# A two-block transformer kernel: modulation in column quarters, attention heads scored in pairs, weights divided ahead of plain transposes

## The chip, the cores and the metric

The kernel runs on one NeuronCore of a Trainium2 chip, as one launch. The metric is the device time of that launch in microseconds. The core has a matrix engine (TensorE, in the profile PE for products and PEld for loading their stationary operand), three engines for elementwise work (VectorE or DVE, ScalarE or ACT, GpSimd or POOL), a queue engine (SyncE or SP) that issues most transfers, and 16 DMA engines. All engines run at the same time and meet at semaphores. Operands lie in SBUF (128 partitions), products land in PSUM: eight banks of 512 fp32 columns for each partition.

## The reference, cut to what matters

Two transformer blocks follow one another, each on 256 tokens of an image (`x`) and 256 of a context (`ctx`) of width 1024. All data is fp32.

```
mod = silu(c) @ w_ada + b_ada                       # (1024) @ (1024 x 9*1024): shift, scale, gate, three times; twice 6*1024 in the second model
h   = rmsnorm(x, g) * (1 + scale) + shift
x   = x + 0.5 * gate * rmsnorm(swiglu(h), g)        # FFN 1, for x and for ctx

# mixer of the first block: window attention (8 heads, 2 key heads, 256 own + 256 context keys) and a gated scan in both directions
s = q @ k.T * 64**-0.5                              # windows of 128 masked
p = softmax(concat(s_band, s_ctx, sink))            # the sink has no value row
o = p @ v
y = (sigmoid(ga) * (o @ w_o_attn) + sigmoid(gh) * (readout(scan) @ w_o_hgrn)) @ w_out

# second model, layer 0: RWKV-7 scans and latent attention (8 heads of 96) on context, then on x; MoE of 16 experts
# second model, layer 1: grouped-query attention (16 heads of 64, 4 key heads) of 256 queries on 512 keys; MoE
p = softmax(q @ k.T * scale);  o = p @ v;  x = x + gate * (o @ w_out)
```

## The kernel before, in words

Weights are read from HBM once, in pieces of 512 KB (`w_raw`, 128 partitions x 1024 fp32 columns, four buffers in most phases). Most products are made with more than one fast product: an operand is split into a rounded part and a remainder (`split`: ScalarE writes `w_hi`, VectorE or POOL writes `w_lo`), and three products of the fast type fp32r are summed in PSUM (`mm3`, L226 to L230). Products that are written with plain fp32 operands (`mm`, L214) are issued as two instructions each.

The phases in order of time are: `p1` with `ab1` inside it (FFN 1 of the first model for context and x, all its modulation, and beside it the RWKV and latent attention of the context in the second model), `p2` (the first mixer: projections, HGRN and window attention as four streams), `p3` (FFN 2), `ab0` (RWKV and latent attention of x, and the modulation of the last layer beside them), a first MoE, `gq` (grouped-query attention), a second MoE.

Streams are Python generators. In `p1`/`ab1`, `p2` and `ab0` they are advanced one step at a time in an order written out by hand as a string (`ORDERS`, where `T` is a step of the filling work, FFN and modulation). Inside that order a planner of the framework places the instructions on the engines by a simulated timeline. On the chip, TensorE and SyncE's queue run theirs in order.

**Modulation** (`ada`, L380 to L413): the vector silu(c) is put into `aT`, 128 x 8 x 32 with two columns in use (x and context). A group of 2048 columns is computed into one PSUM bank: four chunks of 512 columns go to the four strips of 32 partitions (`ps[32 * c:32 * c + 32]`). For each of eight blocks of 128 rows of the weights, two tiles of 1024 columns are loaded, and each tile feeds two chunks. After the eighth block the group is handed over: VectorE adds the bias (`ada_m`), four DMAs write rows to HBM, TensorE transposes four blocks, VectorE copies them (`mt_...`), and bias rows for the next group are loaded into the one buffer `biasr`. The stream has one PSUM buffer (`sm=1`) in `p1`, two in `ab0`. The matrix of 9216 columns makes five groups, the last half full, and each of 6144 makes three: 11.

**Attention** (`attend`, L635 to L687) serves three callers: window attention (`window` in `mixer1`, 8 heads, 512 keys), latent attention (`mla`, 8 heads, once with 256 keys and once with 512), grouped-query attention (`gqa`, 16 heads, 512 keys). For each head and each of two query tiles, `weights` makes scores `at_s` in PSUM by three fp32r products, the maximum `at_mx` (VectorE), the exponential `at_p` with its sum (ScalarE), the reciprocal `at_rd` (VectorE) and a diagonal matrix of it (`diag`, VectorE). `turned` makes, one step later, `at_p` transposed and divided in one go: a product of each 128x128 block with the diagonal (`at_pp`), copied by ScalarE to `at_pt`. After the second tile of an odd head, the values of two heads are summed in `po`, and split into `o_t`.

In window and grouped-query attention a key head holds 64 of the 128 partitions, so its scores are products of 64 rows, in the upper or lower half of the array.

`gq` has four PSUM buffers of one bank each for `acc` and four for `sm`.

Of the kernel before, what the change touches and what calls it, by code (L numbers as in the profile page):

```python
# [132 lines left out]
class _Net:  # L133
    def __init__(self, tc, io, dbg=None):
        self.tc, self.nc, self.io, self.dbg = tc, tc.nc, io, dbg or {}
        self.slots = None
        self.fill = self.wx = None
        self.wn = {"raw": 0, "hi": 0}
# [228 lines left out]
    @contextlib.contextmanager  # L367
    def modulating(self):

        with self.pool("adp", side="right") as self.adp:  # L370
            self.biasr = self.adp.tile([128, 512], F32, name="biasr")
            self.nc.gpsimd.memset(self.biasr, 0.0)
            self.aT = [self.adp.tile([128, 8, 32], F32, name=f"aT{i}") for i in range(2)]
            for i, a in enumerate(self.aT):
                self.nc.vector.memset(a, 0.0)
                self.cp(a[:, :, 0:2], self.vT[:, i * 16:i * 16 + 16].rearrange("p (v k) -> p k v", v=2))
            yield


    def ada(self, pool, which, w, bias, boff, ncols, tag, groups):  # L380


        rows = self.dram([2, ncols], F32, f"ada_{tag}")
        for g in range((ncols + 2047) // 2048):
            c0 = g * 2048
            nch = min(4, (ncols - c0) // 512)
            ps = self.sm()
            for k in range(8):
                raws = []
                for c2 in range(nch // 2):  # L390
                    raw = self.w_raw(2, 512)
                    self.dma(raw.rearrange("p a b -> p (a b)"), w[k * 128:(k + 1) * 128, c0 + c2 * 1024:c0 + (c2 + 1) * 1024])
                    raws.append(raw)
                for c in range(nch):
                    self.mm(ps[32 * c:32 * c + 32, :], self.aT[which][:, k, :], raws[c // 2][:, c % 2, :], k == 0, k == 7)
                if k < 7:
                    yield
            for c in range(nch):
                self.dma(self.biasr[32 * c:32 * c + 2, :], _rep(bias, 2, boff + c0 + c * 512, 512))
            m = self.adp.tile([128, 512], F32, name="ada_m", bufs=1)  # L400
            n = nch * 32
            self.tt(m[:n], ps[:n], self.biasr[:n], OP.add)
            if n < 128:
                self.nc.vector.memset(m[n:], 0.0)
            for c in range(nch):
                self.dma(rows[:, c0 + c * 512:c0 + (c + 1) * 512], m[32 * c:32 * c + 2, :])
            t = pool.tile([128, 4, 4, 2], F32, name=f"mt_{tag}{g}")
            pt = self.sm()
            for blk in range(4):
                self.tr(pt[:, blk * 128:(blk + 1) * 128], m[:, blk * 128:(blk + 1) * 128])  # L410
            self.cp(t, pt.rearrange("p (b c r) -> p b c r", b=4, c=4)[:, :, :, 0:2])
            groups.append((rows, t))
            yield  # L413
# [10 lines left out]
    def pre(self, groups, jshift, jscale, v, gcol):  # L424
        def mod_T(j):
            g, s = divmod(2 * j, 4)
            return groups[g][1][:, :, s:s + 2, v].rearrange("p b c -> p c b")
        gs, sh = self.t(8, name="pre_gs"), self.t(8, name="pre_sh")
        self.cp(sh.rearrange("p (c b) -> p c b", c=2), mod_T(jshift))
        self.stt(gs.rearrange("p (c b) -> p c b", c=2), mod_T(jscale), 1.0,  # L430
                 self.vT[:, gcol:gcol + 8].rearrange("p (c b) -> p c b", c=2), OP.add, OP.mult)
        return gs, sh

    def gate(self, groups, j, v, post=None, scale=1.0, out=None):

        if out is None:
            out = self.t(1024, name="gate")
        rows = groups[0][0]
# [196 lines left out]
    def attend(self, npair, q_of, k_of, v_of, nk, scale, o_t, ok, sink=None, mask=None):  # L635
        nkt = nk // 128

        def weights(h, qt):

            s = self.acc("at_s")  # L640
            self.mm3(s[:, :nk], q_of(h, qt), k_of(h), True, True)
            if mask is not None:
                c0, m = mask(qt)
                self.tt(s[:, c0:c0 + 128], s[:, c0:c0 + 128], m, OP.add)
            mx = self.t(4, name="at_mx")
            self.red(mx[:, 0:1], s[:, :nk], OP.max)
            if sink is not None:
                self.ts(mx[:, 0:1], mx[:, 0:1], scale, sink[:, h:h + 1], OP.mult, OP.max)
                self.ts(mx[:, 1:2], mx[:, 0:1], -1.0, None, OP.mult)
            else:  # L650
                self.ts(mx[:, 1:2], mx[:, 0:1], -scale, None, OP.mult)
            p = self.t(512, name="at_p")
            self.act(p[:, :nk], s[:, :nk], AF.Exp, scale=scale, bias=mx[:, 1:2], accum_out=mx[:, 2:3])
            if sink is not None:
                self.act(mx[:, 3:4], sink[:, h:h + 1], AF.Exp, bias=mx[:, 1:2])
                self.tt(mx[:, 2:3], mx[:, 2:3], mx[:, 3:4], OP.add)
            rd = self.t(1, name="at_rd")
            self.nc.vector.reciprocal(out=rd, in_=mx[:, 2:3])
            return p, self.diag(rd)
        pts = {}  # L660

        def turned(h, qt, p, dg):

            pr, par = divmod(h, 2)
# [6 lines left out]
            if (par, qt) != (1, 1):  # L671
                return
            po = self.sm("po")
            for kt in range(nkt):
                for par in range(2):
                    self.mm(po[64 * par:64 * par + 64, :256], v_of(2 * pr + par, kt), pts[2 * pr + par][:, kt, :], kt == 0, kt == nkt - 1)
            self.split(o_t.pair(ok + pr, 0, 256), po[:, :256])

        was = None
        for h in range(2 * npair):  # L680
            for qt in range(2):
                now = h, qt, *weights(h, qt)
                if was:
                    turned(*was)
                was = now
                yield
        turned(*was)  # L687
# [50 lines left out]
    def mixer1(self, hx, hc, end):  # L738
# [175 lines left out]
        def window():  # L914
# [17 lines left out]
            akT = [self.t(512, dt=F32R, name="akT") for _ in range(2)]  # L932
            self.split(akT, ps)
# [12 lines left out]
            def mask(qt):  # L946
                return (128, self.k["win0"]) if qt == 0 else (0, self.k["win1"])
            yield from self.attend(4, lambda h, qt: [z[64 * (h // 4):64 * (h // 4) + 64, h % 4, qt * 128:(qt + 1) * 128] for z in aqT],
                                   lambda h: [z[64 * (h // 4):64 * (h // 4) + 64, :] for z in akT],
# [462 lines left out]
    def mla(self, ht, keep, is_x, outs):  # L1412
# [126 lines left out]
        yield from self.attend(4, q_of, k_of,  # L1539
# [3 lines left out]
    def gqa(self, ht, hc, x, G):  # L1543
# [79 lines left out]
        for _ in self.attend(8, lambda h, qt: [t[rows(h), h % 4, qt * 128:(qt + 1) * 128] for t in qT[h // 8]],  # L1623
                    lambda h: [t[rows(h), :] for t in kT[h // 8]], lambda h, kt: v[kt][:, h // 4, :], 512, 0.125, o_t, 0):
            pass
        self.proj(o_t, (0, 128), io["gqa_w_out_2"][0], D, [[(0, 512), (512, 512)]], self.gated_to(x, G))
# [278 lines left out]
    def run(self, out):  # L1905
        nc, io = self.nc, self.io
        with contextlib.ExitStack() as es:
# [26 lines left out]
            with self.pool("mods1", side="right") as mods1:  # L1934
# [24 lines left out]
                with self.modulating(), self.pool("zp") as self.zp, self.phase("p1", s=8, h=2, q=2, f=4, b=6, acc=2) as p1:  # L1959
                    ada1 = self.within(self.stream("ada", sm=1), ada1)  # L1960
                    while not m1:
                        next(ada1)
# [14 lines left out]
                    while not m2[0]:  # L1977
                        self.tick()
# [82 lines left out]
    def rest(self, pre2, gate2, x, xc, out, caps, full=None):  # L2061
# [17 lines left out]
        with self.phase("gq" + u, f=17, b=14, q=16):  # L2079

            with self.tc.high_priority(offset=100):
                ht = self.norm_T([(x, lambda: pre2(1, 0, 0))])
            self.gqa(ht, self.norm_T([(xc, lambda: pre2(1, 0, 1))]), x, gate2(1, 0, 0))
            for i in range(2):
                self.dump(f"l1{i}", x[i])
# [33 lines left out]
```

## Time and profile before

| what | value |
|---|---|
| median of three runs | 2508.39 us (2505.49 to 2510.97) |
| profiled execution | 2502.3 us, span 2500.4 us |
| mean granted clock of TensorE | 0.958 of full |
| busy in the span | PE 2287.3, PEld 1795.0, DVE 1448.8, ACT 1151.7, POOL 476.5 us |
| read from HBM | 415.99 MB |

Busy time counts an instruction from its start to its end; products are pipelined, so the starts of two lie closer than one lasts. A line number is that of the listing above, and one that belongs to a helper (L214 for every plain product, L236 for every ScalarE operation) is told apart by the tiles: `out<-in`. "Idle before" is the time in which an engine had nothing to run ahead of these instructions, and what ended it stands behind the arrow.

### The profile page before, as it was taken

To read this page: it belongs to the slowest core of one execution; us is meant where nothing else is said; L and a number is where in the kernel's file an instruction comes from. 1 tells how busy PE (TensorE), PEld (TensorE's weight loads), DVE (VectorE), ACT (ScalarE), POOL (GpSimd) and SP (SyncE) were. 2 spreads that over 40 slices of the span, in tenths; PEclk is the share of its full clock that TensorE was granted. 3 is DMA by queue.
4 is the path that set the end of the run, shared out by engine and by line. 5 is a ranking of instruction groups with operands and counts; after the bars stand their busy time and mean duration, and the time that the engine had idled before them with its cause. 6 is when DMAs were issued, how large, how long until landed. Compare 5 with 4: busy or idle time off the path is not lost. (4 is left out here: it accounts for less than half of the span.)

```text
span 2500.4 us, 42084 instructions
## 1 busy us (share of the span) xinstructions
PE 2287.3 (91%) x16807; PEld 1795.0 (72%) x16807; DVE 1448.8 (58%) x2433; ACT 1151.7 (46%) x1784; POOL 476.5 (19%) x398
## 2 busy tenths in 40 slices
PE   5899999989999989999899899989888978897996
PEld 1686666778888778877799777577676656676774
DVE  1344333466555755786655544554766777547776
ACT  1344223365355434564544453344346754445664
POOL 1132000042000310000100232142225433001342
PEclk9999999999999989999999999989899998898998
DMA  8777776653434433431766556720349983114897
GB/s 275 217 201 235 238 233 226 195 171 119 136 119 135 149 123 101 131 101 45 236 188 185 155 164 197 250 66 18 128 148 340 380 301 105 37 46 152 300 327 245
DMA packets 371414, 445.02 MB, mean 178 GB/s; under 512 B 20928, under 2 KB 273632, under 8 KB 371208
## 3 DMA queue, kind: packets, MB, share of 16 engines
q1 hardware_dynamic: 362280, 409.98, 51.2%
q0 software_dynamic: 4320, 15.47, 1.9%
q10 hardware_dynamic: 4608, 16.78, 1.7%
q8 instruction: 134, 2.20, 0.4%
q14 instruction: 72, 0.59, 0.1%
HBM read 415.99 MB, written 26.96 MB: 177 GB/s over the span
## 5 line engine op out<-in xcount | busy, mean ns | idle before, releaser
L236 ACT ACTIVATE w_hi<-w_raw 128x1024 fp32r<-128x1024 f32 (+2 forms) x550 | 574.8, 1050 | 786.9 <-PE acc L230 313.2
L242 DVE TENSOR_TENSOR w_lo<-w_raw,w_hi 128x1024 fp32r<-128x1024 f32 (+1 forms) x466 | 584.8, 1261 | 457.6 <-ACT w_hi L236 436.1
L228 PE MATMUL acc<-h_h,w_hi 128*128 128x256 f32 (+1 forms) x1392 | 398.0, 286 | 8.0 <-ACT w_hi L236 6.2
L230 PE MATMUL acc<-h_h,w_lo 128*128 128x256 f32 (+1 forms) x1392 | 398.8, 287 | 1.5 <-DVE w_lo L242 0.9
L229 PE MATMUL acc<-h_l,w_hi 128*128 128x256 f32 (+1 forms) x1392 | 390.9, 281 | 0.6 <-POOL h_l L242 0.4
L228 PEld LDWEIGHTS acc<-h_h,w_hi 128*128 128x128 f32 (+1 forms) x1392 | 262.0, 188 | 26.1 <-ACT w_hi L236 10.2
L230 PEld LDWEIGHTS acc<-h_h,w_lo 128*128 128x128 f32 (+1 forms) x1392 | 261.6, 188 | 19.8 <-issue 10.9
L242 POOL TENSOR_TENSOR w_lo<-w_raw,w_hi 128x1024 fp32r<-128x1024 f32 (+1 forms) x84 | 201.9, 2417 | 345.1 <-ACT w_hi L236 331.6
L229 PEld LDWEIGHTS acc<-h_l,w_hi 128*128 128x128 f32 (+1 forms) x1392 | 262.0, 188 | 2.9 <-POOL h_l L242 1.5
L214 PE MATMUL sm<-w_raw,aT 128*32 128x512 f32 x672 | 161.8, 635 | 19.3 <-DMA w_raw<-in_ada_w 8.2
L229 PE MATMUL acc<-w_lo,h_h 128*128 128x512 f32 (+1 forms) x304 | 119.7, 394 | 0.0
L230 PE MATMUL acc<-w_hi,h_l 128*128 128x512 f32 (+1 forms) x304 | 117.1, 390 | 0.0
L229 PE MATMUL acc<-w_lo,mo_e_h 128*128 128x512 f32 x256 | 105.6, 413 | 11.9 <-DVE w_lo L242 11.1
L228 PE MATMUL acc<-w_hi,h_h 128*128 128x512 f32 (+1 forms) x304 | 111.4, 397 | 3.0 <-ACT h_h L236 3.0
L242 POOL TENSOR_TENSOR rs_r<-rs_t,mhalf 128x1 f32<-128x1 f32 (+2 forms) x37 | 38.5, 1041 | 390.8 <-DVE rs_t L246 388.1
L228 PE MATMUL acc<-w_hi,mo_e_h 128*128 128x512 f32 x256 | 104.6, 409 | 3.1 <-ACT w_hi L236 2.5
L229 PE MATMUL acc<-w_lo,f_a_h 128*128 128x512 f32 x264 | 104.8, 403 | 0.0
L228 PE MATMUL acc<-w_hi,f_a_h 128*128 128x512 f32 x264 | 102.9, 412 | 1.7 <-ACT f_a_h L236 1.6
L230 PE MATMUL acc<-w_hi,mo_e_l 128*128 128x512 f32 x256 | 102.2, 399 | 0.0
L230 PE MATMUL acc<-w_hi,f_a_l 128*128 128x512 f32 x264 | 101.3, 397 | 0.0
L214 PEld LDWEIGHTS acc<-ab_Gt,ab_T 64*64 64x64 f32 x1536 | 77.9, 135 | 31.3 <-issue 26.2
L214 PE MATMUL acc<-ab_Gt,ab_T 64*64 64x64 f32 x1536 | 97.7, 224 | 0.0
(542 smaller groups left out, 4471.6 us busy)
## 6 DMA issues: line engine op xcount, KB each, us to landing
w_raw<-in_ffn_w_in SPq DMA_DIRECT2D x132, 512.0 KB
w_raw<-in_ada_w SPq DMA_DIRECT2D x96, 512.0 KB
w_raw<-in_w_ada SPq DMA_DIRECT2D x72, 512.0 KB
w_raw<-in_ffn_w_out SPq DMA_DIRECT2D x66, 512.0 KB
w_raw<-in_moe_w_gate SPq DMA_DIRECT2D x128, 256.0 KB
w_raw<-in_moe_w_up SPq DMA_DIRECT2D x128, 256.0 KB
w_raw<-in_moe_w_down SPq DMA_DIRECT2D x64, 512.0 KB
w_raw<-in_mix_w_in SPq DMA_DIRECT2D x42, 512.0 KB
```

What stands on the lines that cost most here:

```text
L214: self.nc.tensor.matmul(out, lhsT=lhsT, rhs=rhs, start=start, stop=stop, **kw)
L228: mm(out, lhsT=l[0], rhs=r[0], start=start, stop=False)
L229: mm(out, lhsT=l[0], rhs=r[1], start=False, stop=False)
L230: mm(out, lhsT=l[1], rhs=r[0], start=False, stop=stop)
L236: self.nc.scalar.activation(out, in_, f, **kw)
L242: (e or self.nc.vector).tensor_tensor(out=out, in0=a, in1=b, op=op)
```

## The change

Three things are done together. The modulation is computed in groups of 1024 columns, and each weight tile of 1024 columns is cut into four quarters of 256, one for each strip. The buffers and the readers (`pre`, `gate`) follow: group `j` is now the vector `j`, and the places that waited for the first group wait for two. Attention divides the weights by their sum where they lie (`ts` on `at_p`) and turns them with plain transposes in place of products with a diagonal. And `attend` takes a list of pairs of heads and scores them, in grouped-query attention, `together`: both heads of a pair have keys in different halves of the partitions, the scores go to a PSUM tile of two banks (`acc2`), and maximum, scaling and reciprocal are one instruction for two heads. For that the phase `gq` takes two double banks for four single ones, which the projections draw by halves, the pairs of heads are (0,4), (1,5) and so on, and the rows of `w_out` are loaded to match. In window attention each key head gets a tile of its own with the other 64 partitions set to zero, so that its scores are products of 128 rows.

The title of the change also speaks of grouped scan products; no line of the scans (`hgrn`, `rwkv`, `mms`) is in the diff.

```diff
     def acc(self, name="acc"):
+        if self.halves is not None:
+            if not self.halves:
+                t = self.acc2(name)
+                self.halves += [t[:, 1], t[:, 0]]
+            return self.halves.pop()
...
+    def acc2(self, name):
+        p, bufs, tag = self.slots["acc"]
+        return p.tile([128, 2, 512], F32, name=name, tag=tag, bufs=bufs)
...
-        for g in range((ncols + 2047) // 2048):
-            c0 = g * 2048
-            nch = min(4, (ncols - c0) // 512)
+        for g in range(ncols // D):
+            c0 = g * D
             ps = self.sm()
-            for k in range(8):
-                raws = []
-                for c2 in range(nch // 2):
-                    raw = self.w_raw(2, 512)
-                    self.dma(raw.rearrange("p a b -> p (a b)"), w[k * 128:(k + 1) * 128, c0 + c2 * 1024:c0 + (c2 + 1) * 1024])
-                    raws.append(raw)
-                for c in range(nch):
-                    self.mm(ps[32 * c:32 * c + 32, :], self.aT[which][:, k, :], raws[c // 2][:, c % 2, :], k == 0, k == 7)
-                if k < 7:
+            for k in range(0, 8, 2):
+                for kk in range(k, k + 2):
+                    raw = self.w_raw(4, 256)
+                    self.dma(raw.rearrange("p a b -> p (a b)"), w[kk * 128:(kk + 1) * 128, c0:c0 + D])
+                    for c in range(4):
+                        self.mm(ps[32 * c:32 * c + 32, :256], self.aT[which][:, kk, :], raw[:, c, :], kk == 0, kk == 7)
+                if k < 6:
                     yield
...
-            m = self.adp.tile([128, 512], F32, name="ada_m", bufs=1)
+            m = self.adp.tile([128, 256], F32, name="ada_m", bufs=2)
...
-    def attend(self, npair, q_of, k_of, v_of, nk, scale, o_t, ok, sink=None, mask=None):
+    def attend(self, pairs, q_of, k_of, v_of, nk, scale, o_t, ok, sink=None, mask=None, together=False):
...
-            s = self.acc("at_s")
-            self.mm3(s[:, :nk], q_of(h, qt), k_of(h), True, True)
+        def scores(hs, qt):
+            s = self.acc2("at_s") if together else self.acc("at_s")[:, None, :]
+            ops = [(q_of(h, qt), k_of(h)) for h in hs]
+            for n, (a, b) in enumerate(((0, 0), (0, 1), (1, 0))):
+                for z, (l, r) in enumerate(ops):
+                    self.mm(s[:, z, :nk], l[a], r[b], n == 0, n == 2)
...
-            return p, self.diag(rd)
+            for z, p in enumerate(ps):
+                self.ts(p[:, :nk], p[:, :nk], rd[:, z:z + 1], None, OP.mult)
+            return ps
...
-                self.mm(pp[:, kt * 128:(kt + 1) * 128], p[:, kt * 128:(kt + 1) * 128], dg)
+                self.tr(pp[:, kt * 128:(kt + 1) * 128], p[:, kt * 128:(kt + 1) * 128])
...
-            akT = [self.t(512, dt=F32R, name="akT") for _ in range(2)]
-            self.split(akT, ps)
+            akT = [[self.t(512, dt=F32R, name="akT") for _ in range(2)] for _ in range(2)]
+            for z in range(2):
+                r, other = [slice(64 * y, 64 * y + 64) for y in (z, 1 - z)]
+                for k in akT[z]:
+                    nc.gpsimd.memset(k.bitcast(F32)[other], 0.0)
+                self.split([k[r] for k in akT[z]], ps[r])
...
+        pairs = [(8 * z + a, 8 * z + a + 4) for z in range(2) for a in range(4)]
...
-        with self.phase("gq" + u, f=17, b=14, q=16):
+        with self.phase("gq" + u, f=17, b=14, q=16, acc=2):
+            self.halves = []
```

## Rows read from the trace of the kernel before

**Rows 1.** The page's table: busy us (share of the span) x instructions.

```profile
PE 2287.3 (91%) x16807; PEld 1795.0 (72%) x16807; DVE 1448.8 (58%) x2433; ACT 1151.7 (46%) x1784; POOL 476.5 (19%) x398
```

**Rows 2.** Stretches of time: length, busy time by engine, granted clock, DMA share, GB/s.

```profile
0.00:62.00 62.00, 35.03 (x148) 9.96 (x150) 11.56 (x46) 11.32 (x20) 7.67 (x18) 0.92 0.80 275
...
187.00:437.00 250.00, 247.03 (x2098) 165.58 (x2097) 99.92 (x134) 73.52 (x103) 17.12 (x18) 0.99 0.70 233
...
1036.00:1160.00 124.00, 119.25 (x698) 96.90 (x697) 104.64 (x221) 68.41 (x109) 0.53 (x1) 0.96 0.26 83
...
1900.00:2000.00 100.00, 93.44 (x444) 69.10 (x445) 68.85 (x83) 74.67 (x100) 54.16 (x26) 1.00 1.05 380
```

**Rows 3.** Stretches again, TensorE's modulation products alone: busy, clock, DMA, GB/s.

```profile
62.00:500.00 438.00, 94.98 (x384) 0.98 0.70 221
1450.00:1630.00 180.00, 38.37 (x184) 0.98 0.66 210
```

**Rows 4.** Timeline of TensorE: start us, duration us, modulation products and what follows.

```profile
283.89 1.05 PE L214 MATMUL sm<-w_raw,aT 128*32 128x512 f32 x4
284.87 0.27 PE L214 MATMUL sm<-ab_T,ab_Gt 64*64 64x64 f32 x1
...
294.12 1.06 PE L214 MATMUL sm<-w_raw,aT 128*32 128x512 f32 x8
```

**Rows 5.** Waits of SyncE's queue, 187 to 437 us: total, times, longest.

```profile
SPq L211 <- PE sm L214: 105.2, 47, 6.4
```

**Rows 6.** A hand-over on the timeline, and what TensorE waited for before its transposes.

```profile
45.03 0.69 DVE L242 TENSOR_TENSOR ada_m<-sm,biasr 128x512 f32<-128x512 f32 x1 [12.51 <-PE sm L214]
...
46.72 0.64 PE L214 MATMUL sm<-w_raw,aT 128*32 128x512 f32 x4 [0.28 <-DVE mt_a L239]
...
  DVE ada_m L242: 2.7, 2
```

**Rows 7.** Timeline of TensorE in grouped-query attention.

```profile
2161.32 1.94 PE L214 MATMUL po<-at_pt,gq_v 128*64 128x256 f32 x14
...
2163.19 1.16 PE L214 MATMUL at_pp<-diag,at_p 128*128 128x128 f32 x8
2164.28 0.49 PE L228 MATMUL at_s<-gq_kT,gq_qT 64*128 64x512 f32 x1
...
2165.17 1.16 PE L214 MATMUL at_pp<-diag,at_p 128*128 128x128 f32 x8
```

**Rows 8.** Timeline of TensorE: four plain transposes and what follows.

```profile
516.92 0.60 PE L233 MATMUL sm<-tri,mla_q 128*96 128x128 f32 x4
517.45 0.33 PE L214 MATMUL sm<-ab_UV,ab_SC 128*64 128x64 f32 x2
```

**Rows 9.** Timeline of TensorE around one window step (three at_s left out).

```profile
1062.65 0.39 PE L230 MATMUL acc<-w_hi,h_l 128*128 128x512 f32 x1
1062.88 0.40 PE L228 MATMUL acc<-w_hi,h_h 128*128 128x512 f32 x1
...
1064.43 0.39 PE L230 MATMUL acc<-w_hi,h_l 128*128 128x512 f32 x1
```

**Rows 10.** Groups of instructions by form: busy us, mean ns of one | idle before.

```profile
L214 PE MATMUL acc<-ab_lw,ab_lo 64*128 64x512 f32 x16 | 6.9, 861 | 5.0 <-DMA ab_lw<-in_rw_w 4.3 <-DVE ab_sg L242 0.7
```

**Rows 11.** Stretches at the grouped-query stage, columns as in rows 2.

```profile
2134.00:2151.00 17.00, 11.15 (x32) 7.87 (x33) 12.25 (x29) 5.55 (x10) 2.90 (x1) 0.51 0.15 50
2151.00:2232.00 81.00, 81.00 (x472) 56.61 (x471) 35.80 (x131) 43.76 (x102) 0.00 (x0) 1.00 0.01 1
```

**Rows 12.** Stretch by tile (at_pp, then at_s); then min/median/max ns of two scalings.

```profile
2136.00:2232.00 96.00, 37.03 (x256) 31.70 (x256) 18.90 (x32) 0.92 0.02 6
...
2136.00:2232.00 96.00, 32.81 (x96) 17.62 (x96) 21.52 (x32) 24.78 (x64) 0.92 0.02 6
...
L246 DVE TENSOR_SCALAR diag<-tri,at_rd x80: 267/280/830, 552.4 to 2223.0; 128x128 f32<-128x128 f32 x80
...
L246 DVE TENSOR_SCALAR fz<-fz x4: 693/694/695, 956.4 to 959.3; 128x1024 f32<-128x1024 f32 x4
```

More of the change, by code (lines that the diff above doesn't have):

```diff
@@ new lines, in ada @@
+            for k in range(0, 8, 2):
[5 more added lines that the diff above has]
+                if k < 6:
+                    yield
+            for c in range(4):
+                self.dma(self.biasr[32 * c:32 * c + 2, :], _rep(bias, 2, boff + c0 + c * 256, 256))
@@ L408, in ada @@
+            m = self.adp.tile([128, 256], F32, name="ada_m", bufs=2)
+            self.tt(m, ps[:, :256], self.biasr, OP.add)
+            for c in range(4):
+                self.dma(rows[:, c0 + c * 256:c0 + (c + 1) * 256], m[32 * c:32 * c + 2, :])
+            t = pool.tile([128, 2, 4, 2], F32, name=f"mt_{tag}{g}")
             pt = self.sm()
-            for blk in range(4):
+            for blk in range(2):
                 self.tr(pt[:, blk * 128:(blk + 1) * 128], m[:, blk * 128:(blk + 1) * 128])
-            self.cp(t, pt.rearrange("p (b c r) -> p b c r", b=4, c=4)[:, :, :, 0:2])
+            self.cp(t, pt[:, :256].rearrange("p (b c r) -> p b c r", b=2, c=4)[:, :, :, 0:2])
@@ L437, in gate @@
             out = self.t(1024, name="gate")
-        rows = groups[0][0]
+        rows = groups[j][0]
         self.dma(out, _rep(rows, 128, v * rows.shape[1] + j * 1024, 1024))
@@ L654, in weights @@
             if sink is not None:
[L655 to L658, printed above, removed]
-            return p, self.diag(rd)
+                self.act(mx[:, 3, :], sink[:, hs[0]:hs[0] + 1], AF.Exp, bias=mx[:, 1, :])
+                self.tt(mx[:, 2, :], mx[:, 2, :], mx[:, 3, :], OP.add)
+            rd = self.t(m, name="at_rd")
@@ L674, in turned @@
             for kt in range(nkt):
-                for par in range(2):
-                    self.mm(po[64 * par:64 * par + 64, :256], v_of(2 * pr + par, kt), pts[2 * pr + par][:, kt, :], kt == 0, kt == nkt - 1)
+                for par, z in enumerate(pairs[pr]):
+                    self.mm(po[64 * par:64 * par + 64, :256], v_of(z, kt), pts[z][:, kt, :], kt == 0, kt == nkt - 1)
             self.split(o_t.pair(ok + pr, 0, 256), po[:, :256])
[L679 to L687, printed above, removed]
+        if together:
+            order = [(hs, qt) for hs in pairs for qt in range(2)]
+        else:
+            order = [((h,), qt) for hs in pairs for h in hs for qt in range(2)]
+        was = []
+        for hs, qt in order:
+            now = [(h, qt, p) for h, p in zip(hs, weights(hs, qt, scores(hs, qt)))]
+            for z in was:
+                turned(*z)
+            was = now
+            yield
+        for z in was:
+            turned(*z)
     def rope(self, out, x, cs, nh, hd, view=None):
@@ L1538, in mla @@
         om = outs["la"] = self.ht(4, 256, "ab_om")
-        yield from self.attend(4, q_of, k_of,
+        yield from self.attend([(2 * z, 2 * z + 1) for z in range(4)], q_of, k_of,
                     lambda h, kt: keep["v"][kt][:, h, :], nk, 96 ** -0.5, om, 0)
@@ L1976, in run @@
                     self.ab_params(self.zp)
-                    while not m2[0]:
+                    while len(m2[0]) < 2:
                         self.tick()
```

71 lines of the change are left out of this document (36 added, 35 removed).

## The prediction, written before the changed kernel ran

> **What bounds the kernel now.** I read the page's table of engines first: TensorE is busy 91% of the span and no other engine comes near it [rows 1]. A mean over stages decides nothing, so next came the table of stretches [rows 2]. In the first 62 us TensorE is busy 35.03 and the transfers run at 275 GB/s: the kernel waits for weights. From 187 to 437 us TensorE is busy 247.03 of 250 with the transfers at 0.70 of their time: there TensorE is the limit, and work taken off it can shorten the span. From 1036 to 1160 us (window attention beside HGRN and projections) it is busy 119.25 of 124, but VectorE 104.64: a second limit stands right behind. In the grouped-query attention, 2151 to 2232 us, TensorE is busy 81.00 of 81 [rows 11]. So I price every edit in TensorE time, and then ask in each stage how much the next limit lets through.
>
> The profiled execution took 2502.3 us (span 2500.4 and 1.9 around it); the median of the runs is 2508.4, 6.1 above. I sum against 2502.3 and add 6.1 at the end.
>
> **Modulation in column quarters.** Before, a 512 KB weight tile holds 1024 columns as two chunks of 512, and each chunk feeds one 32-column strip of the array, so one tile lights two strips of four. One tile costs 284.87 - 283.89 = 0.98 us [rows 4], and it makes four instructions (an fp32 product is issued as two). Where two tiles arrived together their eight instructions took 1.06 us in all [rows 4]: four strips run side by side at no extra time. After, each tile holds four quarters of 256 columns, so every tile lights all four strips, as that row shows, with half the columns: two passes of about 0.24 us (half of 0.98) and a fixed lead of about 0.07, estimate 0.55 us. Bounds: not under 0.49 (half of 0.98), and not over 0.98 if something else than the streamed columns sets the time. I take 0.55.
>
> How many tiles are alone? From 62 to 500 us there are 384 instructions, 96 tiles, busy 94.98 us; from 1450 to 1630 us 184, 46 tiles, 38.37 us [rows 3]. With s tiles alone at 1.05 us busy and d pairs at 1.06: s + 2d = 96 and s + d = 90 give s = 84, d = 6; the later stretch gives s = 27, d = 10. Alone saves 0.43, a pair loses 0.1: 84 x 0.43 - 0.6 = 35 us, and 27 x 0.43 - 1 = 11 us. Before 62 us weights arrive too slowly for it to matter: 0.
>
> How much of the 46 us gets through? The weights of that stage go through four buffers. SyncE waits 105.2 us of the 250 for modulation products to release one [rows 5], so a quicker product also frees the buffer sooner. The rate must rise from 233 GB/s by about a tenth; the start reaches 275 with these same four buffers, the expert stage 380 with more [rows 2]. I take 70%: 25 and 7 us, together 32 (bounds 0 and 46).
>
> The same edit makes 21 groups of 1024 columns out of 11 of 2048, the last of them half empty. Each group ends with a hand-over: bias addition on VectorE, transposes, copy, four small DMAs out and four in, and the group's products wait for the copy because the stream has one PSUM buffer. An open hand-over holds TensorE 46.72 - 45.03 = 1.69 us; with its blocks halved, about 1.2. But transposes waited for the bias sum in only two cases, 2.7 us in all [rows 6]: in-order TensorE is filled by other streams. The 84 more small DMAs cost SyncE queue time, which has the waiting of [rows 5] to spare. Two more open ones at the start cost 3 us at most, inside the 30% that I held back. If the cover were gone it is the fourth rival.
>
> **Attention weights divided, and plain transposes.** Before, each head and query tile multiplies its weights by a diagonal: four fp32 products in eight instructions, 2164.28 - 2163.19 = 1.09 us [rows 7]. Four plain fp32 transposes are four instructions, 517.45 - 516.92 = 0.53 us [rows 8]. So 0.56 us for each of 64 steps with 512 keys, and half of it for the 16 steps of the context's latent attention with 256. VectorE builds no diagonal (280 ns) but scales 512 columns; that form has no row. Between 128x128 at 280 ns and 128x1024 at 694 ns [rows 12] lies 0.46 us on a straight line; I take it (bounds 0.28 and 0.69): VectorE gains 0.18 us of work a step. The division now stands ahead of the transposes, but these belong to the step before, so it is hidden.
>
> **Grouped-query attention, two heads at once.** Before, per head and tile TensorE spends 0.89 on scores, 1.09 on the diagonal and a quarter of 1.87 on values [rows 7], 2.45 us: 78 us for 32 steps. After, the two heads of a pair sit in the upper and the lower 64 rows of the array. Products of such halves overlap: 16 of mean 861 ns are busy 6.9 us, half their sum of 13.8 [rows 10]. So both heads' scores cost the 0.89 of one, and a pair-step is 0.89 + 0.97 for eight transposes + 0.94 for values = 2.8 us, 45 us for 16. What is late next: ScalarE needs 24.78 / 32 = 0.77 for the exponential and its sum, and 18.90 / 32 = 0.59 for the copy [rows 12], 2.7 us a pair-step and 2.9 with the copies of the output; VectorE about 1.2 + 0.3 + 0.92 + 0.2 = 2.6 (twice the 0.67 of the maximum [rows 12], less one start; two tiny operations, put at one 128x128 scaling; two scalings of 0.46; a share of the output's split, an estimate). Three engines then stand at 42 to 46 us, ScalarE and VectorE also split the output weights, and each pair-step is a chain through all three. Nothing so balanced runs at its bound: I take 3.6 us a pair-step, 58 us, a saving of 20 (bounds 33 at TensorE's 2.8, and 0). The PSUM pairs take the same four banks, and w_out loads in 16 DMAs for 8 while queues are idle: 0.
>
> **Window attention.** The keys of the other group are set to zero and all 128 rows are used. Three 64-row products between full ones stretch five starts to 1064.43 - 1062.88 = 1.55 us where the pitch is 0.23 [rows 9], so changing the row shape costs 1.55 - 1.17 = 0.38 us a step. That goes: 16 x 0.38 = 6 us, with transposes 16 x 0.56 = 9: 15 us of TensorE time. The four clears lie on POOL, busy 0.53 of 124 us [rows 2]. But VectorE, at 104.64 of 124, gets 16 x 0.18 = 3 us more, and two half splits: I let half pass, 7 us (bounds 0, 15).
>
> **Latent attention.** 16 x 0.56 + 16 x 0.28 = 13.5 us beside the RWKV steps; two thirds, 9 us (bounds 0, 13.5). The first words, grouped scan products, name nothing in the diff: no line of HGRN or RWKV products changes: 0.
>
> **Sum.** 32 + 20 + 7 + 9 = 68 us: 2502.3 - 68 = 2434, and 2440 against the median.
>
> **The clock.** The granted clock fell to its lower level, 1.2 GHz, from 2134 to 2151 us, where TensorE was busy 11.15 of 17 us, and stood at 2.4 GHz in the dense 81 us behind [rows 11]. After, TensorE has gaps there. The Trainium skill, "TensorE: Matmul & The Clock Gate" (Part 4: PE-mode transpose), says that transposes do not count as busy in the way that products do and do not bring the full clock. By that rule 128 transposes at 0.13 us, 17 us of the 45, would drop out of what holds the clock, which would speak for the third rival; the transposes of [rows 8] ran quickly, but for half a microsecond, and no run here shows a long stretch of them.
>
> **The rivals.**
> 1. All of TensorE's saving counts: 46 + 33 + 15 + 13.5 = 107 us, 2401. For it: TensorE at 247 of 250 and 81 of 81. Against: VectorE in the window stage, the four buffers. Chance 0.20.
> 2. The weight feed takes the modulation's gain: only 36 us are left, 2472. For it: the first 62 us, bound by transfers at 0.80. Against: 0.70 in the stage. Chance 0.15.
> 3. The grouped-query stage runs at 1.2 GHz: 2 x 2.7 = 5.4 us a pair-step, 86 us in place of 78. 8 us lost where 20 were to be won: 2440 + 28 = 2468. For it: the clock's fall at 2134. Against: TensorE still has over three quarters of that time. Chance 0.08.
> 4. Slower: the hand-overs are no longer covered. Twice as many, each blocking SyncE's in-order queue, with the weight loads of all streams behind the four row DMAs that wait for the bias sum. At 5 us each, the open hand-over and one weight transfer behind it, 21 x 5 = 105, less the 8 that two open ones cost now: 2440 + 97 = 2537. It decides from 3.6 us a hand-over on (68 + 8 over 21). For it: the start is such a place. Against: [rows 6]. Chance 0.07.
>
> My forecast has 0.50; its own range is 2420 to 2460. All but the fourth lie within 2395 to 2485, which also holds the bounds except those where nearly all vanish at once. Two runs of this kernel can be told apart from about 0.2%, 5 us: faster 0.90, the same 0.03, slower 0.07.
>
> **What would show it.** Modulation products of 128x256 at about 0.5 us a tile, eight starts within it; 62 to 500 us shorter by some 25, with more waits of TensorE for w_raw if the second rival holds. 288 transposes instead of 576 diagonal products. In the grouped-query stage pairs of scores that start together, about 60 us, and ScalarE or VectorE as the releaser. Window scores at the plain pitch. The forecast is wrong if the quarters do not overlap, if TensorE's gaps grow as fast as its work shrinks, or if the reordering of a stage by the planner, which I cannot read from this trace, moves more than these terms.

## The result, and the profile after

The changed kernel took 2465.5 us (median of 4 runs, 2463.2 to 2470.9), the kernel before beside it 2506.9: a ratio of 0.9836, 95% interval 0.9815 to 0.9858. The gain is 41 us where 68 were forecast; 2440 was 25 us too low, inside the recorded range and just outside the forecast's own (2420 to 2460). The profiled execution has a span of 2462.6 us.

The page's table first, the answer to [rows 1] (columns as there).

```profile
PE 2201.6 (89%) x17189; PEld 1768.4 (72%) x17189; DVE 1462.5 (59%) x2405; ACT 1149.5 (47%) x1787; POOL 482.1 (20%) x402
```

TensorE lost 86 us of work (2287.3 to 2201.6) and the span only 38: its idle time grew from 213 to 261 us. So most of the parts did on TensorE what was forecast; what failed is how much of it the stages let through. Stretches of the changed kernel, in the order of [rows 2] and [rows 11] (the window stage starts 16 us earlier now):

```profile
0.00:62.00 62.00, 33.80 (x260) 14.28 (x260) 12.47 (x51) 11.57 (x20) 7.00 (x18) 0.91 0.85 290
187.00:437.00 250.00, 230.81 (x2428) 171.81 (x2428) 99.89 (x142) 75.16 (x106) 16.27 (x16) 0.99 0.74 243
1020.00:1144.00 124.00, 110.07 (x653) 90.77 (x652) 107.97 (x223) 69.64 (x111) 1.06 (x2) 0.97 0.27 83
...
2120.00:2130.00 10.00, 7.29 (x30) 4.93 (x31) 8.68 (x19) 4.07 (x9) 0.00 (x0) 0.53 0.00 0
2130.00:2177.00 47.00, 38.25 (x264) 23.49 (x262) 27.19 (x63) 30.45 (x78) 0.00 (x0) 1.00 0.00 1
```

From 187 to 437 us TensorE fell from 247 to 231 of 250 and the transfers rose from 233 to only 243 GB/s. In the window stage it fell from 119 to 110 of 124 while VectorE rose from 105 to 108. The prices per instruction came out as forecast. Timeline of TensorE, modulation first (answer to [rows 4]: one load alone, then two together), then the window's scores between other products (answer to [rows 9]):

```profile
254.19 0.64 PE L224 MATMUL sm<-w_raw,aT 128*32 128x256 f32 x8
254.76 0.27 PE L224 MATMUL acc<-ab_Gt,ab_T 64*64 64x64 f32 x1
...
259.79 1.07 PE L224 MATMUL sm<-w_raw,aT 128*32 128x256 f32 x16
...
1086.77 0.39 PE L240 MATMUL acc<-w_hi,h_l 128*128 128x512 f32 x1
1087.01 0.86 PE L224 MATMUL at_s<-akT,aqT 128*128 128x512 f32 x3
1087.70 1.06 PE L224 MATMUL acc<-hx 128*128 128x128 f32 x8
```

A load alone takes 254.76 - 254.19 = 0.57 us (forecast 0.55, before 0.98), and three full-height scores pass at 0.69 / 3 = 0.23 us, the plain pitch. Over the stretch of [rows 3] the modulation's products fell from 94.98 to 60.06 us, by the 35 of the forecast (first number behind the length):

```profile
62.00:500.00 438.00, 60.06 (x752) 16.78 (x752) 100.14 (x82) 95.23 (x92) 22.16 (x10) 0.97 0.72 226
```

SyncE's waits from 187 to 437 us, the answer to [rows 5]; the first line is one of the kernel before, the others are of the changed kernel:

```profile
SPq L211 <- DVE w_lo L242: 28.1, 15, 4.7
...
SPq L221 <- PE sm L224: 47.4, 30, 4.4
SPq L221 <- DVE w_lo L252: 46.8, 25, 6.7
SPq L221 <- DMA w_raw<-in_w_ada: 22.1, 20, 1.9
...
SPq L221 <- DVE ada_m L252: 12.8, 9, 2.7
```

The wait for the products halved (105.2 to 47.4), and the split of the feed-forward weights that hold the same four buffers took its place (28.1 to 46.8). The hand-overs, hardly in the queue before, cost it 12.8 us.

Stage by stage, from the start times of named tiles in the profiled runs (end of the first modulation stage: `kept<-mla_v`, the first store of the latent values): that end came 16 us earlier (516.1 to 500.1); the latent attention of the context behind it took 355.1 and 356.4 us; the mixer with the window 278.1 and 276.0; the second modulation stage with its latent attention 372.5 and 368.1; the grouped-query stage, first score to router, 132.6 and 116.9.

Such readings have an error of their own. In the four kernels e2, e3, g1 and the changed one, whose code up to the grouped-query attention differs at most in the window's keys, the first end lay at 507.9, 497.4, 501.8 and 500.1 us, and the second modulation stage took 364.8, 360.7, 364.9 and 368.1. A stage whose code is the same moved by up to 10 us. Whether the planner's order or the feed of the run does that, I did not separate. So a difference below some 10 us in these two stages, or below some 4 us in the mixer (275.8 to 279.6 in seven kernels with the same window code), is not a finding here.

### The profile page after: what moved, and what is told of

Same layout as the page of the kernel before. It is cut to its first block, busy times and chain, and to the rows that moved or that the text cites. A ratio compares the mean times of both kernels' runs of the same rounds, so it can differ in the third digit from the quotient of the medians.

```text
span 2462.6 us, 42928 instructions
## 1 busy us (share of the span) xinstructions
PE 2201.6 (89%) x17189; PEld 1768.4 (72%) x17189; DVE 1462.5 (59%) x2405; ACT 1149.5 (47%) x1787; POOL 482.1 (20%) x402
## 5 line engine op out<-in xcount | busy, mean ns | idle before, releaser
L224 PE MATMUL sm<-w_raw,aT 128*32 128x256 f32 x1344 | 113.9, 413 | 23.8 <-DMA w_raw<-in_w_ada 11.0
L240 PE MATMUL acc<-w_hi,h_l 128*128 128x512 f32 (+1 forms) x304 | 116.9, 387 | 0.1
L224 PE MATMUL acc<-ab_Gt,ab_T 64*64 64x64 f32 x1536 | 103.7, 228 | 0.0
```

The lines of the kernel that those rows point to most:

```text
L224: self.nc.tensor.matmul(out, lhsT=lhsT, rhs=rhs, start=start, stop=stop, **kw)
L240: mm(out, lhsT=l[1], rhs=r[0], start=False, stop=stop)
```

## The experiments

Ratios are to the kernel before, timed beside each run. The changed kernel stands at 0.9836.

| run | median us | ratio, 95% interval |
|---|---|---|
| e1, quarters alone | 2488.4 | 0.9915 (0.9892 to 0.9938) |
| e2, heads single | 2477.8 | 0.9887 (0.9867 to 0.9906) |
| e3, half keys | 2468.7 | 0.9856 (0.9838 to 0.9874) |
| e4, diagonal in window and latent | 2465.7 | 0.9833 (0.9809 to 0.9857) |
| m1, half the modulation bytes | 2430.9 | 0.9682 (0.9665 to 0.9699) |
| m1 on the kernel before | 2476.8 | 0.9873 (0.9853 to 0.9893) |
| m3, six raw buffers | 2446.4 | 0.9759 (0.9742 to 0.9776) |
| b3, six buffers on the kernel before | 2470.5 | 0.9877 (0.9856 to 0.9899) |
| w0, no division in window and latent | 2454.5 | 0.9803 (0.9777 to 0.9829) |
| g1, late division | 2455.0 | 0.9788 (0.9768 to 0.9809) |
| c1 = m3 + g1 | 2436.5 | 0.9732 (0.9711 to 0.9753) |
| c2 = c1 + six buffers later | 2432.8 | 0.9716 (0.9692 to 0.9739) |

### What each part is worth

**e1.** The kernel before with the part of the change that lies in `modulating`, `ada`, `pre`, `gate` and the two `while` conditions.

```diff
-        for g in range((ncols + 2047) // 2048):
+        for g in range(ncols // D):
...
-                    self.mm(ps[32 * c:32 * c + 32, :], self.aT[which][:, k, :], raws[c // 2][:, c % 2, :], k == 0, k == 7)
+                        self.mm(ps[32 * c:32 * c + 32, :256], self.aT[which][:, kk, :], raw[:, c, :], kk == 0, kk == 7)
```

> The kernel before with one part of the change: the modulation in four column quarters, nothing of the attention. Recorded sum: 32 us (25 in the first stretch, 7 in the second), so about 2475. Theory A, the parts add up and each pays what the stages of the changed kernel show (the end of the first modulation 16 to 23 us earlier, the second stretch 5 more): 20 to 28 us, 2479 to 2487. Theory B, the gain of the first stretch comes from the new order that the planner writes and not from the products: under 15 us, over 2492.

21 us by the ratio (16 to 27), as theory A has it, though the median stands 1 us above its range. The modulation is half of the whole gain, and 11 us under the forecast's 32.

**e2.**

```diff
-            512, 0.125, o_t, 0, together=True)
+            512, 0.125, o_t, 0)
-        with self.phase("gq" + u, f=17, b=14, q=16, acc=2):
-            self.halves = []
+        with self.phase("gq" + u, f=17, b=14, q=16):
```

> The changed kernel with the grouped-query heads one at a time again: four single banks for the scores, one maximum a head; the division on VectorE and the plain transposes stay. Recorded step: the pairs and their concurrent halves carry the stage's 20 us (the stages show 17), so 2480 to 2486. Rival: the plain transposes carry it, as pairs only put two heads behind one maximum: within 5 us of the changed kernel, 2460 to 2470.

Slower than the changed kernel by 0.0051 of 2507, 13 us, between the two expectations and nearer to the first. First to last score took 84.0 us before, 79.7 here and 65.6 in the changed kernel. These 14 us are not the pairs' alone, as the granted clock (third number from the end) differs, first in e2, then in the changed kernel:

```profile
2115.70:2195.40 79.70, 70.24 (x308) 40.74 (x308) 46.95 (x138) 41.57 (x95) 2.90 (x1) 0.82 0.02 4
```

```profile
2111.00:2176.60 65.60, 47.72 (x304) 29.43 (x304) 42.62 (x94) 38.73 (x94) 2.90 (x1) 0.90 0.04 9
```

In e2 the first 28 us of the stage ran at the lower level, in the changed kernel 14 us, in the kernel before 15; e1, whose attention is that of the kernel before, had 27. So how long this lasts varies with the same code. Where the clock stood at 1.00, two heads took 4.9 us before, 4.6 in e2 and 4.1 in the changed kernel, from one maximum to the next. By these steps, 16 times, the pairs are worth some 8 us and the transposes with division some 4 to 5; the rest of the 14 falls into the part at the lower level. The changed stage then loses some 3 us behind the last score (2176.6 to 2227.9, against 2220.5 to 2269.1 before), so some 16 of the forecast 20 reach the router.

**e3.** The window's keys as before; queries and keys of a head are again the 64 rows from 64 * (h // 4).

```diff
-            akT = [[self.t(512, dt=F32R, name="akT") for _ in range(2)] for _ in range(2)]
...
+            akT = [self.t(512, dt=F32R, name="akT") for _ in range(2)]
+            self.split(akT, ps)
```

> The changed kernel with the window's keys in 64-row halves again instead of whole tiles padded with zeros. Recorded step: six of its seven window us are the row-shape switch, so 4 to 6 us slower, 2470 to 2472. Rival, VectorE is the window stage's limit and TensorE's saving there reaches nothing: within 2 us, 2463 to 2468.

0.9856 against 0.9836 is 5 us, but the intervals overlap: not settled.

**e4.**

```diff
+            if not together:
+                return [(ps[0], self.diag(rd))]
...
+                if together:
+                    self.tr(pp[:, kt * 128:(kt + 1) * 128], p[:, kt * 128:(kt + 1) * 128])
+                else:
+                    self.mm(pp[:, kt * 128:(kt + 1) * 128], p[0][:, kt * 128:(kt + 1) * 128], p[1])
```

> The changed kernel in which the weights of the window and of the two latent attentions are turned by the product with the diagonal of the reciprocals again (no division on VectorE there); the grouped-query stage keeps division and transposes. Recorded sum: nine of the latent us and part of the window's seven come from the transposes, so 9 to 14 us slower, 2474 to 2480. Rival, those stages are held by VectorE, where a diagonal (280 ns) is cheaper than a division of 128x512 (some 440 ns) 48 times over: within 3 us or faster, 2458 to 2468.

No difference (0.9833), as the rival has it, though the time alone does not show the rival's reason. Of the forecast 9 us of the latent attention, and the transposes' part of the window's 7, nothing shows; the two intervals leave room for some 8 us.

### Why the window and the latent attention gained nothing

**w0.**

```diff
-                self.ts(p[:, :nk], p[:, :nk], rd[:, z:z + 1], None, OP.mult)
+                if together:
+                    self.ts(p[:, :nk], p[:, :nk], rd[:, z:z + 1], None, OP.mult)
```

> The changed kernel without the division of the weights by their sums in the window and the two latent attentions (48 operations of 128x512 on VectorE less; the output is left wrong there); transposes and the rest stay. Theory, VectorE holds these stages and the division took there what the transposes saved TensorE: 6 to 12 us faster than the changed kernel, 2453 to 2460. Rival, the scans and hand-overs beside the attention hold the stages and neither the transposes nor the division are on their path: within 3 us, 2462 to 2469.

8 us faster by the ratios, whose intervals overlap a little. The stage says where. The mixer with the window, from its first gate `fz` to the last merged tile: the kernel before, the changed kernel, and without division (columns as in [rows 2]).

```profile
921.80:1199.90 278.10, 272.79 (x1509) 223.64 (x1508) 191.54 (x338) 137.11 (x195) 2.15 (x4) 0.98 0.32 98
```

```profile
907.10:1183.10 276.00, 261.55 (x1445) 215.41 (x1444) 193.94 (x339) 136.63 (x197) 3.20 (x6) 0.99 0.33 99
```

```profile
909.20:1178.20 269.00, 259.32 (x1445) 215.56 (x1444) 188.31 (x323) 136.97 (x197) 3.21 (x6) 0.99 0.31 102
```

Before to after, TensorE's work falls by 11.2 us and the stage by 2.1. Without the division TensorE's work hardly moves, VectorE's falls by 5.6, and the stage is 7 shorter. In six more kernels with the same window code (e2, m1, m3, g1, c1, c2) it took 275.8 to 279.6, in e3 280.1 and in e4, with diagonals, 280.3. So the division lies on the path that holds this stage, a path through VectorE as [rows 2] had warned, and it put back what the transposes took. VectorE is not full there (193.94 of 276.00 us), so the path is a chain and not a busy engine. It does not hold the context's latent attention: that took 356.4 us with division, 356.0 without, 355.7 with the diagonal. Neither form is on its path. What is, I did not isolate; the scan's hand-overs stand beside it all the way. The latent attention of x lies in the second modulation stage, which took some 359 us without the division, 364 with the diagonal and 368 in the changed kernel: hardly more than that stage's error, so not settled.

### Where the modulation's gain went

**m1.**

```diff
-  self.dma(raw.rearrange("p a b -> p (a b)"), w[kk * 128:(kk + 1) * 128, c0:c0 + D])
+  self.dma(raw[:, 0:2, :].rearrange("p a b -> p (a b)"), w[kk * 128:(kk + 1) * 128, c0:c0 + 512])
...
-  raw[:, c, :], kk == 0, kk == 7)
+  raw[:, c % 2, :], kk == 0, kk == 7)
```

> The changed kernel with half of the modulation's weight bytes left out: each load brings 512 of its 1024 columns and the four products of a tile use these twice, so that part of the output is left wrong; instructions and their number stay. Theory A, the feed of weights holds back the first stretch (TensorE fell from 48 to 50 us in 50 to 41 to 48, the loads' share is 0.74): 8 to 18 us faster than the changed kernel, 2447 to 2458. Rival B, what is left there are dependences between engines (TensorE waiting for the split weights of ScalarE and for the mixer's chains), not the transfers: within 4 us, 2461 to 2469.

> The same with the kernel before: each 1024-column load of the modulation brings 512 of them, used twice, and part of the output is left wrong. Theory A: the kernel before is full of TensorE there (48 to 50 us in 50), so fewer bytes give it nothing or little: 2500 to 2508. If instead it gains as much as the changed kernel does, the feed was a limit all along and not one that the quarters uncovered: 2488 to 2498.

The changed kernel gains 0.0154, 39 us, far over theory A's 18. The kernel before gains 0.0127, 31 us: my own expectation for it failed, and the second sentence holds. The feed was a limit before the change too, in a stage where TensorE read 97% busy. With half the bytes the change is worth 0.9873 - 0.9682 = 0.0191, 48 us, against 41; with an error of some 9 us on the difference, these two are not told apart.

**m3 and b3.** A pool `wx` of two more raw tiles, open over `p1` with `ab1` in it, so over the first stage and the latent attention behind it (in b3 also `m = self.biasr` for the tile `ada_m`, to make room).

```diff
+XR = 2
...
-                with self.modulating(), self.pool("zp") as self.zp, self.phase("p1", s=8, h=2, q=2, f=4, b=6, acc=2) as p1:
+                with self.modulating(), self.pool("zp") as self.zp, self.phase("p1", s=8, h=2, q=2, f=4, b=6, acc=2) as p1, \
+                        self.pool("wx", reuse_waits="tile") as self.wx:
+                    self.xr = XR
...
-        p, n = self.w_pool("raw", 3)
+        p, n = self.w_pool("raw", self.xr)
```

> The changed kernel with six instead of four buffers for raw weights in the first stretch (modulation, first feed-forward, first mixer), all else as it is. If the feed is held by buffers that come free late (SyncE waited 47 us there for products to free one): 5 to 12 us faster, 2453 to 2460. If it is held by the rate of the transfers themselves or by the split of the weights on ScalarE and VectorE behind them, six buffers give 0 to 4 us: 2461 to 2466.

> The kernel before with six instead of four raw weight buffers in the first stretch (to make room, the modulation's sums are added into the bias rows' tile). The changed kernel became 18 to 20 us faster by these. If four buffers held both kernels alike, the kernel before gains as much, 12 to 20 us, 2488 to 2496, and the change is still worth 41 to 46 us. If the column quarters uncovered that limit, it gains 8 us at most, over 2500, and with enough buffers the change is worth 54 us or more.

m3 gains 0.0077, 19 us: the buffers, more strongly than expected. b3 gains even more, 31 us, so neither of its expectations was right: the four buffers held the kernel before harder than the changed one. With six, the change is worth 0.9877 - 0.9759 = 0.0118, 30 us instead of 41, a difference just over its error of some 9 us. The first stage from 62 us to its end (columns as in [rows 2]), for the kernel before, b3, the changed kernel, m3, and the two with half the bytes, before and changed:

```profile
62.00:516.10 454.10, 440.52 (x3437) 318.20 (x3434) 191.22 (x257) 159.69 (x231) 52.13 (x48) 0.98 0.69 220
```

```profile
62.00:484.10 422.10, 414.65 (x3378) 310.59 (x3377) 188.87 (x250) 155.29 (x222) 52.51 (x46) 1.00 0.73 235
```

```profile
62.00:500.10 438.10, 407.26 (x3801) 322.94 (x3802) 191.86 (x265) 161.55 (x233) 53.41 (x48) 0.97 0.72 226
```

```profile
62.00:481.00 419.00, 400.16 (x3788) 322.46 (x3785) 190.12 (x261) 160.94 (x229) 52.47 (x47) 0.98 0.76 242
```

```profile
62.00:489.10 427.10, 421.44 (x3346) 307.66 (x3345) 186.78 (x249) 154.08 (x220) 50.80 (x46) 1.00 0.57 172
```

```profile
62.00:470.30 408.30, 399.15 (x3739) 315.94 (x3739) 188.64 (x260) 159.51 (x230) 51.95 (x47) 1.00 0.60 181
```

And TensorE's modulation products up to 520 us (count, busy us, mean ns of one | idle before) in the kernel before, b3 and the changed kernel:

```profile
L214 PE MATMUL sm<-w_raw,aT 128*32 128x512 f32 x480 | 122.4, 645 | 17.2 <-DMA w_raw<-in_w_ada 7.0 <-DMA w_raw<-in_ada_w 6.2 <-DVE rs_t L246 3.5
```

```profile
L216 PE MATMUL sm<-w_raw,aT 128*32 128x512 f32 x480 | 106.9, 624 | 13.1 <-DMA w_raw<-in_w_ada 10.9 <-DMA w_raw<-in_ada_w 1.9 <-DVE mt_a L241 0.3
```

```profile
L224 PE MATMUL sm<-w_raw,aT 128*32 128x256 f32 x960 | 83.1, 424 | 19.8 <-DMA w_raw<-in_w_ada 11.0 <-DMA w_raw<-in_ada_w 4.8 <-DVE rs_t L256 3.3
```

Read the first two numbers of each stretch as length and TensorE's work. Before to after: work -33.3, as forecast (35), length -16.0: 48% got through, the rest is idle time, 13.6 to 30.8 us. With half the bytes: work -22.3, length -18.8, 84%. With six buffers (b3 to m3): work only -14.5, length -3.1. These shares are of single executions and carry the stage's error. In e1, with the same quarters, the work fell by 27.9 and the length by 9.6, 34%:

```profile
62.00:506.50 444.50, 412.64 (x3827) 326.25 (x3820) 193.46 (x270) 161.82 (x234) 53.44 (x48) 0.97 0.72 225
```

They also leave out the first 62 us, in which the six kernels above had TensorE busy 35.03, 37.10, 33.80, 35.25, 41.75 and 38.86 us; counted from the start, 46%, 75% and 19% got through. So it is shown that the feed holds both kernels (31 and 39 us with half the bytes); that it took the missing part of the modulation's gain fits the shares and the waits, but is not shown beyond the error.

The old products themselves had become cheaper in b3, 122.4 to 106.9 us, because more loads stood ready in twos, and two together cost the old form what one alone does [rows 4]. On the timeline from 62 to 520 us the kernel before has 72 loads alone and 10 pairs, b3 37 alone and 19 pairs. So four buffers made loads come singly, which is what the quarters repair; that they also kept TensorE from using what the quarters saved is argued from the waits for the split weights. What still leaves m3 18.8 us of idle time there is open; its transfers stand at 0.76 of their time.

### The grouped-query step, and a faster kernel

**g1.** In `attend`, for pairs, the reciprocal and the division are wrapped and called after the next pair's `weights`.

```diff
+            if together:
+                late.append(divide)
...
             now = [(h, qt, p) for h, p in zip(hs, weights(hs, qt, scores(hs, qt)))]
+            if was and late:
+                late.pop(0)()
```

> The changed kernel in whose grouped-query stage the division of one pair's weights is written behind the maximum of the next pair, so that VectorE works while ScalarE takes the exponentials. Theory, the stage is a ping-pong of the two engines (maximum 1.20, factor 0.16, two exponentials 1.5, division 0.9, 3.9 to 4.1 us a pair-step) where each waits for the other: a step falls to some 2.9 us, what ScalarE has to do in it, 16 times, so 12 to 17 us faster, 2448 to 2454. Rival, TensorE's own work of a step (scores 0.97, transposes 1.09, values and the hand-overs between them) or the planner's order set the 3.9 us: within 4 us, 2461 to 2468.

12 us by the ratios, as the theory's lower end. The timeline of the changed kernel, one pair-step (start, duration, and in brackets the wait and what ended it):

```profile
2143.30 0.96 PE L224 MATMUL at_s<-gq_kT,gq_qT 64*128 64x512 f32 x6 [0.64 <-ACT at_p L246]
...
2145.52 0.69 ACT L246 ACTIVATE at_p<-at_s,at_mx 128x512 f32<-128x512 f32 x1 [0.82 <-DVE at_mx L256]
...
2147.00 0.17 DVE L672 RECIPROCAL at_rd<-at_mx 128x2 f32<-128x2 f32 x1 [1.57 <-ACT at_p L246]
2147.08 1.20 DVE L262 TENSOR_REDUCE at_mx<-at_s 128x2 f32<-128x1024 f32 x1
...
2147.09 0.98 PE L224 MATMUL at_s<-gq_kT,gq_qT 64*128 64x512 f32 x6
...
2148.20 0.87 DVE L256 TENSOR_SCALAR at_p<-at_p,at_rd 128x512 f32<-128x512 f32 x2
...
2149.33 0.16 DVE L256 TENSOR_SCALAR at_mx<-at_mx 128x2 f32<-128x2 f32 x1
2149.58 0.69 ACT L246 ACTIVATE at_p<-at_s,at_mx 128x512 f32<-128x512 f32 x1 [1.36 <-DVE at_mx L256]
...
2150.14 1.09 PE L243 MATMUL at_pp<-tri,at_p 128*128 128x128 f32 x8
```

Step to step 2149.58 - 2145.52 = 4.06 us. The reciprocal waits 1.57 us for the exponentials on ScalarE, and the next pair's maximum (2147.08) stands behind it in VectorE's order, though the scores that it reads, those of 2143.30, were done at 2144.26 (the scores of 2147.09 start with it and are for the pair after). Then ScalarE waits 1.36 for VectorE. VectorE's waits in the stage, the changed kernel and g1 (total, times, longest):

```profile
DVE at_rd L672 <- ACT at_p L246: 20.9, 13, 2.0
```

```profile
DVE gq_o_l L252 <- ACT gq_o_h L246: 5.0, 4, 1.5
DVE at_mx L262 <- PE at_s L224: 3.7, 7, 1.0
...
DVE at_rd L674 <- ACT at_p L246: 0.2, 1, 0.2
```

20.9 us of waiting became 0.2 and first to last score took 53.3 us instead of 65.6.

**c1 and c2.** c1 joins m3 and g1; c2 opens two more raw tiles over the second modulation stage too, in the same way.

> The changed kernel with both: six raw weight buffers in the first stretch, and the division of the grouped-query pairs behind the next pair's maximum. They lie in stages apart, so their 19 and 12 us add: 2432 to 2438. If one is given back at the stage border or by the planner's order: 2440 to 2447.

> The kernel of both edits with six raw buffers also in the second modulation stretch (the mixer's second call). Halving the modulation's bytes took some 4 us off that stretch, so the feed is worth little there: 0 to 5 us beyond the kernel of both, 2428 to 2437. If that stretch is held by the scan's chains alone: no difference.

Both are faster than the kernel before and than the changed one. c1 gains 0.0104, 26 us, on the changed kernel, a little under the sum of its parts (31) and inside its range; c2 is 0.9716 (0.9692 to 0.9739), 30 us, and not to be told from c1.

## Why the prediction was right, and where its sizes were off

The direction and most prices of single operations were right; the shares that the stages let through were too high, by about 11 us in the modulation, 4 in grouped-query attention, 5 in the window and 9 in the latent attention. The measured 2465.5 lies nearer to the second rival's 2472 and the third's 2468 than to 2440, but neither of their mechanisms made it: e1 alone gains 21 us where the second rival leaves the modulation nothing, and the third is answered under the clock.

- **Prices of single operations.** Right: 0.57 us for a load (0.55), 1.09 us for eight transposes (0.97, where twice the sum's own 0.53 for four makes 1.06), 0.87 for two divisions on VectorE (0.92), 0.96 to 0.98 for a pair's scores (0.89). The sum worked out 84 loads alone and 6 pairs; the timeline has 72 and 10, and the work fell by the 35 us all the same.
- **The share let through, 70% of the modulation's 46 us.** This is the mis-sized term: 21 us measured alone (e1) for 32, and 34 to 48% in the first stage. The step argued that a quicker product frees its buffer sooner and that the rate need rise only by a tenth. The wait for products did halve, but the next holder of the same buffers, the split of other streams' weights, was right behind it, and the rate rose by 4%, 233 to 243 GB/s. The second rival was true at most in part: the feed holds the stage, but did not take all.
- **All of TensorE's saving (first rival).** TensorE lost 86 us for the 107 forecast, and the span less than half of that. The stages with a second limit did not pay out in full.
- **Hand-overs.** Their cover held: the fourth rival did not happen. They cost SyncE 12.8 us of queue from 187 to 437 us; what of that reaches the end was not tried. The 8 us that the fourth rival took off for two open ones stand in no row; [rows 6] has 2.7.
- **Grouped-query attention.** 20 forecast, some 16 in the stage. The 3.6 us a pair-step were mostly 3.7 to 4.5 at the full clock, 4.1 in the mean. The stage was said to be a chain through three balanced engines; it was a chain, but of VectorE and ScalarE in one avoidable order.
- **Window.** 7 forecast, 2.1 in the stage, inside the error. The second limit was named and then let half of the saving pass; e4 shows no gain from the transposes with division, and w0 that the division itself is on the path.
- **Latent attention.** 9 forecast, nothing (e4). "Two thirds" rested on no row: no wait was shown that the shorter product would have ended.
- **The clock.** Granted at 0.53 while TensorE had gaps, from 2120 to 2130 us, it stood at 1.00, the upper level of 2.4 GHz, from 2130 to 2177, with TensorE busy 38 of 47 us. The third rival, the lower level all through the stage, did not happen; only the stage's beginning ran at it, as in the kernel before. The Trainium skill, "TensorE: Matmul & The Clock Gate" (Part 4: PE-mode transpose), has transposes not count as busy; this trace shows full clock from 2130 to 2177 with 13.3 of the 38 us in them, and holds no long stretch of transposes alone:

```profile
L243 PE MATMUL at_pp<-tri,at_p 128*128 128x128 f32 x96 | 13.3, 280 | 3.0 <-DVE at_p L256 2.5 <-DVE gq_o_l L252 0.5
```

- **Grouped scan products.** Nothing in the diff, nothing in the stages.

## What to carry to other kernels

An engine at 97% busy is no proof that it is the limit: halve the bytes, or add a buffer, before pricing its work at full value, since starved loads made the products dearer here, too. Two more buffers for the raw weights were worth 19 us here and 31 in the kernel before; the latter is three quarters of what the whole change brought. In a chain of two in-order engines, look for an instruction that waits for the other engine with ready work behind it, and write that work first.

## What was not expected of the hardware

- In the kernel before, halving the modulation's bytes shortened the first stage by 27 us (516.1 to 489.1) though TensorE had read 440.5 of 454.1 us busy behind the first 62 us. Some 7 of the 27 us lie in those 62, where it was busy 41.75 instead of 35.03. Behind them its gaps shrank from 13.6 to 5.7 us, and busy time hid both dearer products (122.4 against 116.6 us) and a clock of 0.98 against 1.00:

```profile
0.00:62.00 62.00, 41.75 (x199) 15.64 (x200) 14.40 (x49) 14.60 (x23) 7.60 (x18) 0.92 0.71 214
```

```profile
L214 PE MATMUL sm<-w_raw,aT 128*32 128x512 f32 x480 | 116.6, 633 | 12.6 <-DMA w_raw<-in_w_ada 6.8 <-DMA w_raw<-in_ada_w 5.7
```
